# Building one-hot rows on another engine, turning a product's layout in PSUM, and keeping more low parts in DRAM

## The chip, the cores and the metric

One core of one Trainium2 chip runs the whole kernel. The metric is device time in microseconds (us) of one execution. Before the change the median is 3289.25 us (3288.27 and 3289.25 in two runs of three; a third gave 9417.04). The profiled execution took 3298.0 us, of which the trace spans 3296.2 us.

## The reference

One decoder layer over 1024 tokens of width 1024: a mixer of two branches (RG-LRU and gated linear attention), a projection and a layer norm, then a PEER layer (product keys over 128 x 128 = 16384 single-neuron experts, 8 heads, 16 experts a head) beside a gated projection of per-layer embeddings, and a second layer norm.

```python
z = x @ w_in;  m = sigmoid(g_A) * y_A + sigmoid(g_B) * y_B
x = layer_norm(ALPHA * x + m @ w_out)
ple = sigmoid(x @ W_pg) * (p @ W_pp)
top_s, top_i = top_k(scores of 2 x 128 half keys, 16)          # per head
best_s, best_pos = top_k(16 x 16 sums, 16); gate = softmax(best_s)
hid = gelu(x . u[expert]);  ffn = sum over 128 slots of gate * hid * v[expert]
x = layer_norm(ALPHA * x + ffn + ple)
```

Everything is float32 in and out.

## The kernel before

The tokens go through the mixer and what follows it in two halves of 512 (`mixer(0)`, `post(0)`, `mixer(1)`, `post(1)`), and then `dense` ends the program. Each large product is made of three products of rounded halves (`mm3`, L263 to L265): an operand is split into a high part (ScalarE, L259) and a low part (VectorE subtraction, L260). `weights` (L267 to L287) does this for every weight block, once in each half. The first 60 low parts are also written to DRAM (L286) in the first half and read from there in the second half (L277), where only the high part is then made (L278). In the second half the remaining ones, four blocks of `w_out` (`mix`), eight of the queries (`pq`), eight of the embedding gate (`plg`) and four of its projection (`plp`), are split again.

The experts are computed in two ways. Four of the eight tiles of 128 tokens gather rows of `u` and `v` by indirect DMAs from the GpSimd queue: `gather_u` (L841) takes one expert per token and slot, and VectorE multiplies and sums it (L849); `gather_v` (L857) takes the 128 experts of one token, and TensorE sums them with a weight tile `w32` that is zero but for one column per token (L866, L869). The rows go round in a ring of 7 tiles, 11 later on. The other four tiles are dense: `dense` multiplies them by all 16384 experts, a group of 512 at a time, and multiplies the hidden values by a gate matrix (`gt`, L1042) that lies in DRAM as `g_d`.

`dense_gates` (L962 to L994) builds that matrix while `post(1)` runs. For one token the 128 slots lie on the partitions. One one-hot matrix marks each slot's first key and is scaled by the slot's gate (`oi`), the other marks its second key (`oj`), and their product over the slots (L988) gives 128 x 128 gates. A group is 8 tokens: one VectorE instruction makes eight bare rows of first keys (`one`, L979), one makes eight of second keys (`oj`, L981), ScalarE scales `one` token by token into `oi` (L987), TensorE makes eight products into two PSUM tiles, and ScalarE copies each tile to `gst` with tokens turned innermost (L990). Sixteen tokens go to DRAM in one store (L992). There are 64 groups.

The order of the work: the code is written in one order, and gather work is woven in by `pump`, which hands out a fixed amount of it after each product. A scheduler with its own timing model then orders the instructions of every engine. Each engine, and each of the two DMA queues (SyncE's and GpSimd's), takes its instructions in that order. `dense` may start before the gates are finished, but its first use of the gate matrix (L1042) needs the last store.

## Time and profile before

| What | before |
|---|---|
| median of the runs | 3289.25 us |
| profiled execution | 3298.0 us |
| its span | 3296.2 us |
| TensorE busy | 3042.8 us (92%) |
| VectorE busy | 2375.3 us (72%) |
| ScalarE busy | 1228.2 us (37%) |
| GpSimd busy | 1160.8 us (35%) |
| moved by DMA | 939.74 MB, mean 285 GB/s |

Shares of the whole span hide stages that differ. The program has five: the first mixer, the rest of the first half (some 440 to 640 us), the second mixer (to 1100), the rest of the second half with the gates (1100 to 1632), the dense experts (1632 to 3257), and a tail. A stage is read by its own row of busy times, and then by the waits inside it. Busy time of TensorE counts a matmul longer when the granted clock is low.

### The profile page before, as it was taken

How to read it: one execution, taken by the hardware profiler on the slowest of the kernel's cores; microseconds unless marked ns; L12 is line 12 of the kernel's file. 1: busy time of each engine (PE TensorE's matmuls, PEld its weight loads, DVE VectorE, ACT ScalarE, POOL GpSimd, SP SyncE). 2: the span in 40 equal slices, each digit the busy share in tenths (PEclk: the TensorE clock that was granted, in tenths of full speed). 3: DMA queues.
4: the chain of work that ended last, by engine and by line, in shares of the span. 5: the costliest groups of instructions: out<-in, count | busy, mean ns of one | idle time of the engine just before them, and what ended most of it. 6: DMA issues, size and time to landing. Idle time of an engine off the chain costs nothing.

```text
span 3296.2 us, 48127 instructions
## 1 busy us (share of the span) xinstructions
PE 3042.8 (92%) x17160; PEld 2320.6 (70%) x17160; DVE 2375.3 (72%) x5791; ACT 1228.2 (37%) x2130; POOL 1160.8 (35%) x1034
## 2 busy tenths in 40 slices
PE   8999989797999888658799999999999999999996
PEld 6788777676777676548577777777777777777663
DVE  7556557977888898978887866666666667666333
ACT  6433323263244464648623322222232232223221
POOL 0000000534421445540155444444434545443453
PEclk9999989898999998879899999999999999999997
DMA  5444444777776898976799899999899999988997
GB/s 174 143 172 148 135 160 142 277 293 284 295 263 244 326 312 302 349 252 216 246 376 352 321 338 327 340 338 344 314 340 326 355 335 326 338 328 327 346 322 277
DMA packets 364304, 939.74 MB, mean 285 GB/s; under 512 B 33920, under 2 KB 115968, under 8 KB 359968
## 3 DMA queue, kind: packets, MB, share of 16 engines
q0 software_dynamic: 147456, 536.94, 44.8%
q1 hardware_dynamic: 216608, 399.74, 34.8%
q8 instruction: 134, 2.20, 0.3%
q14 instruction: 106, 0.87, 0.1%
HBM read 854.76 MB, written 81.79 MB: 284 GB/s over the span
## 4 chain that ended last, share of the span: by engine, by line
PE 70%; DVE 14%; DMA 7%; ACT 4%; issue 3%; POOL 1%; SPq 0%; POOLq 0%; DVEq 0%; ACTq 0%
PE ph L263 7%; PE ph L265 7%; PE pv L265 7%; PE pv L263 7%; PE pv L264 7%; PE ph L264 7%; PE ffn L883 7%; DVE ug L849 3%; DMA ug<-in_peer_u_dram,idx 3%; DMA vg<-in_peer_v_dram,idxT 1%; DVE one L979 1%; DVE oj L981 1%; PE pgr L263 1%; PE pgr L264 1%; PE pgr L265 1%
## 5 line engine op out<-in xcount | busy, mean ns | idle before, releaser
L847 POOL DMA_INDIRECT ug<-in_peer_u_dram,idx x512 | 601.3, 1174 | 1345.1 <-DVE bs L776 612.3
L876 POOL DMA_INDIRECT vg<-in_peer_v_dram,idxT x512 | 558.2, 1090 | 756.7 <-DVE ug L849 324.3
L849 DVE SCALAR_TENSOR_TENSOR ug<-ug,x1g 128x1024 f32<-128x1024 f32 x512 | 619.8, 1219 | 47.0 <-DMA ug<-in_peer_u_dram,idx 42.9
L263 PE MATMUL ph<-x1hl,uh 128*128 128x512 f32 x1024 | 408.6, 399 | 0.9 <-DVE sc L737 0.9
L265 PE MATMUL ph<-x1hl,ul 128*128 128x512 f32 x1024 | 407.9, 398 | 0.0
L264 PE MATMUL ph<-x1hl,uh 128*128 128x512 f32 x1024 | 406.6, 397 | 0.0
L264 PE MATMUL pv<-vl,wdh 128*128 128x512 f32 x1024 | 400.5, 393 | 0.0
L263 PE MATMUL pv<-vh,wdh 128*128 128x512 f32 x1024 | 384.3, 393 | 15.9 <-ACT wdh L259 15.9
L265 PE MATMUL pv<-vh,wdl 128*128 128x512 f32 x1024 | 398.7, 393 | 0.0
L259 ACT ACTIVATE uh<-ur 128x512 fp32r<-128x512 f32 x256 | 160.2, 628 | 498.0 <-PE ph L264 489.2
L883 PE MATMUL ffn<-vg,w 128*32 128x512 f32 x2048 | 274.1, 628 | 51.1 <-DMA vg<-in_peer_v_dram,idxT 50.2
L259 ACT ACTIVATE vh<-vr 128x512 fp32r<-128x512 f32 x256 | 160.7, 629 | 356.9 <-PE pv L265 348.7
L260 DVE TENSOR_TENSOR ul<-ur,uh 128x512 fp32r<-128x512 f32 x256 | 175.7, 687 | 159.6 <-ACT uh L259 158.1
L260 DVE TENSOR_TENSOR vl<-vr,vh 128x512 fp32r<-128x512 f32 x256 | 176.3, 690 | 115.2 <-ACT vh L259 115.0
L1062 DVE SCALAR_TENSOR_TENSOR acc<-acc,pv 128x512 f32<-128x512 f32 x256 | 165.0, 681 | 108.8 <-PE pv L265 108.8
L263 PEld LDWEIGHTS pv<-vh,wdh 128*128 128x128 f32 x1024 | 192.8, 188 | 69.3 <-ACT wdh L259 16.1
L263 PEld LDWEIGHTS ph<-x1hl,uh 128*128 128x128 f32 x1024 | 192.4, 188 | 68.6 <-issue 22.6
L265 PEld LDWEIGHTS ph<-x1hl,ul 128*128 128x128 f32 x1024 | 192.4, 188 | 62.1 <-issue 16.8
L265 PEld LDWEIGHTS pv<-vh,wdl 128*128 128x128 f32 x1024 | 192.6, 188 | 58.7 <-issue 16.8
L264 PEld LDWEIGHTS ph<-x1hl,uh 128*128 128x128 f32 x1024 | 192.4, 188 | 55.7 <-issue 11.7
L264 PEld LDWEIGHTS pv<-vl,wdh 128*128 128x128 f32 x1024 | 192.9, 188 | 53.9 <-issue 10.1
L988 PE MATMUL pg<-oi,oj 128*128 128x128 f32 x1024 | 163.2, 301 | 35.9 <-ACT oi L987 25.4
(475 smaller groups left out, 6030.9 us busy)
## 6 DMA issues: line engine op xcount, KB each, us to landing
ur<-in_uT_dram SPq DMA_DIRECT2D x256, 256.0 KB, 6.3
vr<-in_peer_v_dram SPq DMA_DIRECT2D x256, 256.0 KB, 6.3
g_d<-gst SPq DMA_DIRECT2D x32, 1024.0 KB, 8.6
gt<-g_d SPq DMA_DIRECT2D x32, 1024.0 KB, 8.4
raw_zx<-in_w_z_dram SPq DMA_DIRECT2D x16, 512.0 KB, 4.9
raw_zv<-in_w_v_dram SPq DMA_DIRECT2D x16, 512.0 KB, 5.0
raw_zy<-in_w_z_dram SPq DMA_DIRECT2D x16, 512.0 KB, 6.4
raw_ga<-in_w_z_dram SPq DMA_DIRECT2D x16, 512.0 KB, 5.4
```

The lines of the kernel that those rows point to most:

```text
L259: nc.scalar.activation(h, src, AF.Copy)
L260: nc.vector.tensor_tensor(l, src, h, op=ALU.subtract)
L263: nc.tensor.matmul(o, wh, xh, start=first, stop=False)
L264: nc.tensor.matmul(o, wh, xl, start=False, stop=False)
L265: nc.tensor.matmul(o, wl, xh, start=False, stop=last)
L847: nc.gpsimd.indirect_dma_start(out=ug, out_offset=None, in_=a["peer_u"], in_offset=bass.IndirectOffsetOnAxis(ap=idx[:, s:s + 1], axis=0))
L849: nc.vector.scalar_tensor_tensor(ug, ug, 1.0, x1, op0=ALU.mult, op1=ALU.mult, accum_out=hid[:, s:s + 1])
L876: nc.gpsimd.indirect_dma_start(out=vg, out_offset=None, in_=a["peer_v"], in_offset=bass.IndirectOffsetOnAxis(ap=idxT[:, t:t + 1], axis=0))
L883: mm = nc.tensor.matmul(ffn[32 * c:32 * c + 32, e * 512:(e + 1) * 512], w32[:, c, r], rows_v[c][:, e * 512:(e + 1) * 512], start=ph == 0 a ...
L979: nc.vector.tensor_tensor(one, iota, Tb[:, 0, tt, None].to_broadcast(B3), op=ALU.is_equal)
L988: nc.tensor.matmul(o[:, r], oj[:, t], oi, start=True, stop=True)
L1062: nc.vector.scalar_tensor_tensor(acc[c][:, es], acc[c][:, es], 0.5 if g == 0 else 1.0, o[c], op0=ALU.mult, op1=ALU.add)
```

## The change

Five edits:

1. `oi` is made by VectorE, one instruction a token, which compares a row of key numbers with the slot's first key and multiplies by its gate, both read from one column of `T2`. ScalarE no longer makes it.
2. `one` now marks the second key and is laid key, token (128 x 8) so that both inputs and the output are bfloat16 with neighbouring elements next to each other. ScalarE turns it into `oj` (token, key, float32) with one instruction a group. VectorE's `oj` is gone.
3. The product of a token goes into every fourth column of its PSUM tile, which is laid key, token (128 x 4). The copy to `gst` then reads PSUM as it lies and writes four neighbouring values at a time.
4. In `gather_v` the zero fill of `w32` moves from VectorE to GpSimd, and its four small copies move to ScalarE.
5. `LOW = 60` is gone. All low parts but those of the queries (`OWN`) are kept in DRAM: 16 more writes in the first half and 16 more reads in the second, in place of 16 subtractions.

```diff
-LOW = 60
+OWN = ("pq",)
...
-            if key not in low:
-                n = len(low)
-                low[key] = None
-                if n < LOW:
-                    low[key] = dram.tile(shape, F32, name=f"low{n}")
-                    nc.sync.dma_start(low[key], l.bitcast(F32))
+            if name not in OWN and key not in low:
+                low[key] = dram.tile(shape, F32, name=f"low{len(low)}")
+                nc.sync.dma_start(low[key], l.bitcast(F32))
...
-            nc.vector.memset(w32, 0.0)
+            nc.gpsimd.memset(w32, 0.0)
             for c in range(4):
...
-                nc.vector.tensor_copy(dst, pw[:, 32 * c + ph * N:32 * c + ph * N + N])
+                nc.scalar.activation(dst, pw[:, 32 * c + ph * N:32 * c + ph * N + N], AF.Copy)
...
-                one = g_b.tile(B3, BF16, name="one", bufs=2)
-                nc.vector.tensor_tensor(one, iota, Tb[:, 0, tt, None].to_broadcast(B3), op=ALU.is_equal)
-                oj = g_b.tile(B3, F32, name="oj", bufs=2)
-                nc.vector.tensor_tensor(oj, iota, Tb[:, 1, tt, None].to_broadcast(B3), op=ALU.is_equal)
+                one = late.tile([P, KEYS, TG], BF16, name="one", tag="k_", bufs=2)
+                nc.vector.tensor_tensor(one, iota, Tb[:, None, t0:t0 + TG].to_broadcast([P, KEYS, TG]), op=ALU.is_equal)
+                oj = g_b.tile([P, TG, KEYS], F32, name="oj", bufs=2)
+                nc.scalar.activation(oj.rearrange("p t k -> p k t"), one, AF.Copy)
+
+                oi = g_b.tile([P, TG, KEYS], F32, name="oi", bufs=2)
+                for t in range(TG):
+                    nc.vector.tensor_scalar(oi[:, t], iota128, T2[:, 0, t0 + t:t0 + t + 1], T2[:, 1, t0 + t:t0 + t + 1],
+                                            op0=ALU.is_equal, op1=ALU.mult)
                 for r4 in range(TG // 4):
-                    o = gps.tile([P, 4, KEYS], F32, name="pg", tag="g")
+                    o = gps.tile([P, KEYS, 4], F32, name="pg", tag="g")
                     for r in range(4):
                         t = 4 * r4 + r
-                        oi = g_b.tile([P, KEYS], F32, name="oi", bufs=6)
-                        nc.scalar.activation(oi, one[:, t], AF.Copy, scale=T3[:, 2, t0 + t:t0 + t + 1])
-                        nc.tensor.matmul(o[:, r], oj[:, t], oi, start=True, stop=True)
+                        nc.tensor.matmul(o[:, :, r], oj[:, t], oi[:, t], start=True, stop=True)
                     q4 = q * TG + 4 * r4
-                    nc.scalar.activation(gs[:, :, q4:q4 + 4].rearrange("p i t -> p t i"), o, AF.Copy)
+                    nc.scalar.activation(gs[:, :, q4:q4 + 4], o, AF.Copy)
```

The scheduler orders the changed program anew. On VectorE, among the queries of the second half, a piece of the gates read as follows (`list` and `sc_st` belong to the top 16 of the scores, `ug` is a gathered row):

```order
1988 L979 TENSOR_TENSOR one<-iota,Tb 128x1024
1989 L737 MATCH_REPLACE sc_st<-list_11488,sc_st 128x128 x2
1990 L739 MAX_INDEX list_11488<-list_11488,sc_st 128x8
1991 L737 MATCH_REPLACE sc_st<-list_11488,sc_st 128x128
1992 L849 SCALAR_TENSOR_TENSOR ug,hid<-ug,x1g 128x1024
1993 L737 MATCH_REPLACE sc_st<-list_11488,sc_st 128x128
1994 L260 TENSOR_TENSOR wl_pq<-raw_pq,wh_pq 128x1024
1995 L981 TENSOR_TENSOR oj<-iota,Tb 128x1024
```

The same place of the changed kernel:

```order
2028 L981 TENSOR_SCALAR oi<-iota_145,T_11591 128x128 x8
2029 L975 TENSOR_TENSOR one<-iota,Tb 128x1024
2030 L846 SCALAR_TENSOR_TENSOR ug,hid<-ug,x1g 128x1024
2031 L734 MATCH_REPLACE sc_st<-list_11408,sc_st 128x128 x4
2032 L732 MAX list_11408<-sc_st 128x8 x4
2033 L981 TENSOR_SCALAR oi<-iota_145,T_11591 128x128 x6
2034 L735 MAX list_11408<-sc_st 128x8 x4
```

Where a group had two instructions of 1024 elements, it now has one of 1024 and eight of 128, in runs of up to eight.

On ScalarE, further on in the same stage, the gates stood so:

```order
762 L990 ACTIVATE gst<-pg 128x4x128
763 L987 ACTIVATE oi<-one,T_13031 128x128 x4
764 L990 ACTIVATE gst<-pg 128x4x128
765 L987 ACTIVATE oi<-one,T_13031 128x128 x4
766 L990 ACTIVATE gst<-pg 128x4x128
```

And now:

```order
679 L977 ACTIVATE oj<-one 128x128x8
680 L989 ACTIVATE gst<-pg 128x128x4
681 L977 ACTIVATE oj<-one 128x128x8
682 L989 ACTIVATE gst<-pg 128x128x4
683 L977 ACTIVATE oj<-one 128x128x8
684 L989 ACTIVATE gst<-pg 128x128x4
```

Eight scalings and two copies of a group have become one turning copy and two copies.

On TensorE, at the end of the gates, the first products of the dense stage (`ph`) were mixed with the last of the gates (`pg`); 96 of them stood ahead of the last piece:

```order
6146 L264 MATMUL ph<-x1hl,uh 128x512
6147 L265 MATMUL ph<-x1hl,ul 128x512
6148 L988 MATMUL pg<-oi,oj 128x128 x36
6149 L263 MATMUL pv_15402<-vh,wdh 128x512
6150 L264 MATMUL pv_15402<-vl,wdh 128x512
```

In the changed kernel none does:

```order
6026 L264 MATMUL pplp_14634<-wl_plp,Ehl 128x256
6027 L265 MATMUL pplp_14634<-wh_plp,Ehl 128x256
6028 L987 MATMUL pg<-oi,oj 128x128 x8
6029 L263 MATMUL ph<-x1hl,uh 128x512
6030 L264 MATMUL ph<-x1hl,uh 128x512
```

The dense stage's products now follow the last product of the gates, and 36 of them stand ahead of the first `pv`.

## Rows read from the trace of the kernel before

**Rows 1.** Windows by stage: length, busy us (instructions) of each engine, clock, DMA

```profile
440.00:640.00 200.00, 164.98 (x1072) 147.53 (x1073) 155.74 (x589) 49.61 (x80) 30.35 (x24) 0.88 0.52 176
1100.00:1632.00 532.00, 408.26 (x2702) 335.69 (x2701) 477.53 (x1342) 340.70 (x771) 204.90 (x158) 0.88 0.86 291
1632.00:3257.00 1625.00, 1625.00 (x7725) 1171.16 (x7724) 1073.01 (x2134) 457.61 (x767) 765.86 (x713) 1.00 0.92 335
3257.00:3296.00 39.00, 9.59 (x53) 1.75 (x49) 17.07 (x27) 1.36 (x5) 4.69 (x5) 0.56 0.62 228
```

**Rows 2.** Groups by line, VectorE, 1100 to 1632 us: busy, mean ns | idle before

```profile
L849 DVE SCALAR_TENSOR_TENSOR ug<-ug,x1g 128x1024 f32<-128x1024 f32 x81 | 98.3, 1219 | 22.8 <-DMA ug<-in_peer_u_dram,idx 20.5 <-issue 2.1
L981 DVE TENSOR_TENSOR oj<-iota,Tb 128x1024 f32<-128x1024 bf16 x64 | 77.7, 1214 | 4.6 <-PE pg L988 4.6
L979 DVE TENSOR_TENSOR one<-iota,Tb 128x1024 bf16<-128x1024 bf16 x64 | 77.6, 1212 | 13.4 <-ACT oi L987 13.3
L260 DVE TENSOR_TENSOR wl_plg<-raw_plg,wh_plg 128x1024 fp32r<-128x1024 f32 x8 | 9.7, 1213 | 0.5 <-ACT wh_plg L259 0.4
```

**Rows 3.** Groups by line, ScalarE, 1100 to 1632 us

```profile
L987 ACT ACTIVATE oi<-one,T 128x128 f32<-128x128 bf16 x512 | 165.0, 390 | 41.2 <-DVE one L979 21.1 <-PE pg L988 19.9
L990 ACT ACTIVATE gst<-pg 128x512 f32<-128x512 f32 x128 | 133.3, 1054 | 14.0 <-DMA g_d<-gst 9.6 <-PE pg L988 4.2
L683 ACT ACTIVATE sc_st<-psc 128x512 f32<-128x512 f32 x16 | 8.8, 595 | 4.2 <-DVE list L739 4.2
```

**Rows 4.** Waits of TensorE and its weight loads, 1100 to 1632 us: total, times, longest

```profile
PE ffn L883 <- DMA vg<-in_peer_v_dram,idxT: 39.6, 9, 12.2
PE pgb L265 <- DMA wl_gb<-low: 1.1, 1, 1.1
...
PEld pg L988 <- ACT oi L987: 46.6, 45, 4.7
```

**Rows 5.** Groups by line, whole span: shapes that the change uses

```profile
L260 DVE TENSOR_TENSOR vl<-vr,vh 128x512 fp32r<-128x512 f32 x256 | 176.3, 690 | 115.2 <-ACT vh L259 115.0
L809 DVE TENSOR_TENSOR eq<-rb,iota 128x1024 bf16<-128x1024 bf16 x32 | 22.0, 688 | 0.5
L866 DVE MEMSET w<- 128x512 f32 x32 | 15.5, 485 | 26.1 <-PE ffn L883 25.2
```

**Rows 6.** Timeline of VectorE: start, length; 128 elements, constants in the instruction

```profile
575.36 0.22 DVE L785 TENSOR_SCALAR rk<-bp 128x128 uint32<-128x128 uint32 x1
575.49 0.22 DVE L786 TENSOR_SCALAR rk<-bp 128x128 uint32<-128x128 uint32 x1
```

**Rows 7.** Timeline of VectorE: L166 reads a value per partition, 32 elements

```profile
3.60 0.17 DVE L162 TENSOR_SCALAR ish<-irow 128x32 int32<-128x32 int32 x1
3.71 0.24 DVE L166 TENSOR_SCALAR lmask<-i_f,jf 128x32 f32<-128x32 f32 x1
3.87 0.15 DVE L167 TENSOR_SCALAR jsh<-jsh 128x1 int32<-128x1 int32 x1
```

**Rows 8.** Timeline of TensorE: gate products, and two products of the dense stage

```profile
1126.19 2.02 PE L988 MATMUL pg<-oi,oj 128*128 128x128 f32 x16 [0.94 <-DVE oj L981]
...
3210.40 0.39 PE L263 MATMUL ph<-x1hl,uh 128*128 128x512 f32 x1
3210.63 0.39 PE L264 MATMUL ph<-x1hl,uh 128*128 128x512 f32 x1
```

**Rows 9.** Timeline at the end of the gates

```profile
1611.28 1.07 PE L988 MATMUL pg<-oi,oj 128*128 128x128 f32 x6 [0.60 <-ACT oi L987]
...
1628.21 0.80 PE L263 MATMUL pv<-vh,wdh 128*128 128x512 f32 x1 [15.86 <-ACT wdh L259]
```

**Rows 10.** Waits, whole span: the store of the gated embeddings

```profile
ACT tge L716 <- DMA base_d<-tge: 26.0, 3, 15.7
```

**Rows 11.** The chain that ended last, its tail: start, length, what

```profile
3262.25 11.20 DMA vg<-in_peer_v_dram,idxT
3273.49 3.69 PE ffn L883 x16
```

More of the change, by code (lines that the diff above doesn't have):

```diff
@@ L967, in dense_gates @@
             nc.tensor.transpose(o[:, j], K3[:, j], ident)
-        T3 = g_b.tile([P, 3, P], F32, name="T3", bufs=2)
-        nc.scalar.activation(T3, o[:, :3], AF.Copy)
-        Tb = g_b.tile([P, 2, P], BF16, name="Tb", bufs=2)
-        nc.scalar.activation(Tb, o[:, :2], AF.Copy)
+        T2 = g_b.tile([P, 2, P], F32, name="T2", bufs=2)
+        nc.scalar.activation(T2, o[:, 0:3:2], AF.Copy)
+        Tb = g_b.tile([P, P], BF16, name="Tb", bufs=2)
+        nc.scalar.activation(Tb, o[:, 1], AF.Copy)
         for tb in range(P // 16):
@@ L975, in dense_gates @@
                 t0 = tb * 16 + q * TG
-                tt = slice(t0, t0 + TG)
-                B3 = [P, TG, KEYS]
-                one = g_b.tile(B3, BF16, name="one", bufs=2)
-                nc.vector.tensor_tensor(one, iota, Tb[:, 0, tt, None].to_broadcast(B3), op=ALU.is_equal)
-                oj = g_b.tile(B3, F32, name="oj", bufs=2)
-                nc.vector.tensor_tensor(oj, iota, Tb[:, 1, tt, None].to_broadcast(B3), op=ALU.is_equal)
+                one = late.tile([P, KEYS, TG], BF16, name="one", tag="k_", bufs=2)
[6 more added lines that the diff above has]
+                                            op0=ALU.is_equal, op1=ALU.mult)
                 for r4 in range(TG // 4):
-                    o = gps.tile([P, 4, KEYS], F32, name="pg", tag="g")
+                    o = gps.tile([P, KEYS, 4], F32, name="pg", tag="g")
                     for r in range(4):
                         t = 4 * r4 + r
-                        oi = g_b.tile([P, KEYS], F32, name="oi", bufs=6)
-                        nc.scalar.activation(oi, one[:, t], AF.Copy, scale=T3[:, 2, t0 + t:t0 + t + 1])
-                        nc.tensor.matmul(o[:, r], oj[:, t], oi, start=True, stop=True)
+                        nc.tensor.matmul(o[:, :, r], oj[:, t], oi[:, t], start=True, stop=True)
                     q4 = q * TG + 4 * r4
-                    nc.scalar.activation(gs[:, :, q4:q4 + 4].rearrange("p i t -> p t i"), o, AF.Copy)
+                    nc.scalar.activation(gs[:, :, q4:q4 + 4], o, AF.Copy)
                     pump(0.9)
@@ L1106 @@
         gps = gctx.enter_context(tc.tile_pool(name="gps", bufs=3, space=PSUM))
-        iota = late.tile([P, TG, KEYS], BF16, name="iota", tag="tr")
-        nc.scalar.activation(iota, iota128[:, None, :].to_broadcast([P, TG, KEYS]), AF.Copy)
+        iota = late.tile([P, KEYS, TG], BF16, name="iota", tag="tr")
+        nc.scalar.activation(iota, iota128[:, :, None].to_broadcast([P, KEYS, TG]), AF.Copy)
         def all_gates():
```

## The prediction, made before the run

> **What bounds the kernel now.** I read the windows by stage first [rows 1]. From 1632 to 3257 us TensorE is busy for all of 1625 us at full clock: whatever is taken off VectorE, ScalarE or GpSimd there is worth nothing, and the edits of `w32` fall there for the most part. The stage that can give time back is the one with the gates, 1100 to 1632 us. TensorE is busy for 408 of its 532 us, ScalarE for 341, GpSimd for 205, and VectorE for 478. So VectorE bounds it on average, with 54 us of idle time, and TensorE has 124 us in which it waits.
>
> The groups and waits of that stage say for what. VectorE's idle time is 20.5 us of waiting for gathered rows, and 13.3 and 4.6 us before `one` and `oj` for ScalarE and TensorE to give a buffer back [rows 2]. TensorE's weight loads wait 46.6 us for ScalarE's `oi`, and its sums wait 39.6 us for gathered rows [rows 4]. ScalarE spends 165.0 + 133.3 = 298 of its 341 us on `oi` and `gst` [rows 3]. There are thus two things in the way, not one: VectorE's total, and ScalarE as the slow link between VectorE's rows and TensorE's products.
>
> **VectorE's part of the gates.** A group has `one` and `oj`, 1212 and 1214 ns [rows 2], 2.43 us. Now `one` has the shape, types and neighbouring elements of the comparison at L809, 0.69 us [rows 5]. Each `oi` is an instruction of 128 elements that reads two values per partition. No row shows exactly that. With constants in the instruction, 128 elements start 0.13 us apart [rows 6]; that is the lower end. Reading one value per partition lengthens an instruction of 32 elements from 0.17 to 0.24 us, and the next starts after 0.16 us [rows 7]; 96 more elements, at the rate that the 0.22 us of 128 elements against 0.17 us of 32 gives, add 0.05 us. That makes 0.24 + 0.05 = 0.29 us if nothing overlaps, the upper end, and 0.16 + 0.05 = 0.21 us if it overlaps as rows 7 do, which I take because they are the nearest. A group: 0.69 + 8 x 0.21 = 2.37 us against 2.43, so **-4 us** in 64 groups, with **-45 us** (0.13) and **+37 us** (0.29) as ends. VectorE's share of the gates hardly gets smaller; it changes shape.
>
> **ScalarE's part.** A group costs 8 x 0.390 + 2 x 1.054 = 5.23 us [rows 3]. The copy to `gst` writes every value 64 bytes from the last, and took 1054 ns where a copy of the same size that writes neighbours took 595 [rows 3]. I price the new `oj`, twice the size and with steps of 512 bytes, at 2 x 1.054 = 2.1 us (2 x 0.595 = 1.2 us below), and the new `gst`, four neighbours at a time, at 0.595 (1.054 above): 3.3 us a group, between 2.4 and 4.2. In 64 groups ScalarE gives up some 124 us (66 to 181) of its 341. All of it lies beside VectorE's work, so it counts only by the waits that it ends: VectorE's 13.3 + 4.6 us [rows 2], **-18 us**. TensorE's 46.6 us for `oi` go too, but are not added, since VectorE's rows come no sooner.
>
> **Low parts.** In the second half 12 splits of 1024 elements (1.213 us, [rows 2]) and four of 512 (0.690, [rows 5]) leave VectorE: **-17 us**, in the stage that it bounds. In their place SyncE's queue gets 16 reads, 7.3 MB by their shapes. Such reads made TensorE wait 1.1 us once in this stage [rows 4]; I take **+2 us** for 16. In the first half the queue gets 16 writes, next to the stores of `base_d`. The transfers have room there (a share of 0.52, [rows 1]), but the queue is taken in order, and a store that is late holds up ScalarE, which already waited 26.0 us for it [rows 10]. Below nothing; above, each write puts off what stands behind it by its 0.5 MB at 335 GB/s [rows 1], 16 x 1.5 = 24 us. I take **+5 us**: TensorE waits 35 of 200 us there, so not all is hidden.
>
> **`w32`.** Some five of the 32 zero fills lie in this stage (161 of 1024 sums stand ahead of the gates' end in either order), 5 x 0.485 [rows 5] = **-2 us**. The small copies I leave out. GpSimd has 327 us free there, and the fill's wait for a buffer is one that the gather behind it has too: with 11 row tiles, neither goes ahead before the same sum is done. In the dense stage GpSimd is busy for 766 of 1625 us and ScalarE for 458 [rows 1]; a copy that waits on ScalarE delays the splits behind it, which TensorE's loaded blocks cover by some microseconds. If that cover were gone, the 27 later fills would show as gaps in a TensorE that has none.
>
> **Order.** No dense product stands ahead of the last gate any more, so 14 of VectorE's dense splits (0.690, [rows 5]) and some seven dot products (1.219, [rows 2]) move behind it: **-18 us** before that point, into a stage where VectorE has room. In return TensorE had done 96 products at 0.23 us [rows 8], 22 us of work, before the last gate; it then sat idle for 15.9 us [rows 9] until the store, the load of `gt` and `w` were through. Now it can fill that wait with what it had done ahead: I take 5 us of idle time left, so 22 - 15.9 + 5 = **+11 us**. In the tail, 24 sums stood behind the last `pv` and 8 do now: two batches, at half of the 3.69 us that 16 took [rows 11], **-4 us**.
>
> **The sum.** -4 - 18 - 17 + 2 + 5 - 2 - 18 + 11 - 4 = -45 us. One thing pushes back: the same gathers in less time. The stage moves 291 GB/s at a share of 0.86 where the dense stage reaches 335 at 0.92 [rows 1], so 532 x 291 / 335 = 462 us is the least that its transfers allow. They do not bind, but VectorE's 20.5 us of waiting for rows will grow; by half, **+10 us**. Together -35 us. The profiled execution took 3298.0 us, 8.75 above the median of 3289.25, and by its own time would come to 3263. Put to the median, **3254 us**.
>
> **Rivals.**
> - *VectorE takes back what ScalarE gives up.* If eight `oi` in a run do not overlap (0.29 us), VectorE has 41 us more and the sum is +6: 3295 us. For it: the 0.15 to 0.24 us that each instruction takes even when it has almost nothing to do [rows 7], and eight where there were none. Against: every row in the list starts before the one ahead has ended. Chance 0.22.
> - *The values per partition cost nothing.* At 0.13 us: -41 more, 3213 us. For it: rows 6. Against: rows 7. Chance 0.15.
> - *TensorE becomes the bound and the kernel slower.* A gate product now writes every fourth column. 16 halves of products took 2.02 us [rows 8], so one starts every 0.116 us, and there are 1024. TensorE has 124 us of waiting, of which 44 for rows and low parts would stay; the other 80 cover a spacing of up to 0.116 + 80/1024 = 0.19 us, and from there it decides. At twice, 0.232 us, it lacks 39 us: 3289 + 39 + 5 - 4 = 3329 us, if the edits of VectorE give nothing more. Against: a dense product writes 512 neighbouring columns in 0.23 us [rows 8], two in the 0.9 ns in which a gate product writes one, so the gate product leaves each write twice the time. For it: no row shows a spread write. Chance 0.08.
> - *The reads of low parts end nothing because VectorE has other work that holds the same step.* Then the -17 us fall away: 3271 us. Chance 0.05.
>
> [...]
>
> **How the numbers follow.** The forecast, 3254 us, has 0.5, with some 20 us either way for the terms that I only took. The range reaches to the ends of `oi`'s price and 5 us past the upper one, for the terms taken: **3213 to 3300 us**, which leaves out the third rival and what lies past either end, 2 in 10. A difference of 2% (66 us) is about what can be told from no change, so faster is below 3223: most of the second rival and the low edge of the forecast, **0.17**. Slower is above 3355: only a spread write at more than twice the spacing, **0.03**. Within: **0.80**.
>
> **What would show it.** In the profile after: `oi` on VectorE at about 0.29 us busy one by one and 0.21 from start to start; `one` at 0.69; `oj` on ScalarE at about 2 us and `gst` near 0.6; TensorE's `pg` still 0.116 us apart; no wait of `pg` for ScalarE of more than a few microseconds; VectorE as busy as before in the gates' stage, which ends some 40 us sooner, with a stage of 1625 us behind it that has not changed. Wrong would be: gaps in TensorE in the dense stage, `pg` spaced wider, or a first half that is longer by more than 10 us.

## The result, and the profile after

The changed kernel took **3309.89 us** (median of 7 runs), the kernel before beside it 3295.72: the ratio is **1.0053** (95% interval 1.0036 to 1.0070). It is slower by 0.5%, far from the 2% that counts as a difference, and outside the forecast range of 3213 to 3300. The ratio compares the means and leaves out one slow run of the kernel before, of 9417.04 us. A second measurement gave 1.0027 (1.0014 to 1.0040): the sign holds, the size varies. The profiled execution took 3316.68 us with a span of 3314.9, 18.7 us more than the span before.

The steps of the stage can be read from one view, by tile: count, ns of one (min/median/max), first and last start. After:

```profile
L987 PE MATMUL pg<-oi,oj x1024: 270/275/582, 1135.5 to 1594.2; 128*128 128x128 f32 x171
L265 PE MATMUL pplp<-wh_plp,Ehl x64: 276/281/415, 566.1 to 1592.4; 128*128 128x256 f32 x64
L263 PE MATMUL pv<-vh,wdh x1024: 387/389/747, 1638.0 to 3290.2; 128*128 128x512 f32 x171
L880 PE MATMUL ffn<-vg,w x2048: 592/592/1062, 1081.6 to 3293.7; 128*32 128x512 f32 x187
```

(`pg` are the gate products, `pplp` those of the embeddings, `pv` the first of the dense stage that use the gates, `ffn` the sums of gathered rows.) Before, the first gate product started at 1126.2 us, the last at 1612.1, the first `pv` at 1628.2 [rows 8, 9], and the last embedding product at 1542.7:

```profile
L265 PE MATMUL pplp<-wh_plp,Ehl x64: 276/279/415, 564.9 to 1542.7; 128*128 128x256 f32 x64
```

The 18.7 us are then:

| stretch | before | after | difference | forecast |
|---|---|---|---|---|
| up to the first gate product | 1126.2 | 1135.5 | +9.3 | +5 |
| first to last gate product | 485.9 | 458.7 | -27.2 | -47 |
| last gate product to first `pv` | 16.1 | 43.8 | +27.7 | +7 with the next row |
| first `pv` to the end | 1668.0 | 1676.9 | +8.9 | |
| sum | | | +18.7 | -35 |

The gates do end 18 us sooner. The hand-over to `dense` takes all of that back and more. Two windows of before (columns as in [rows 1]), from the first gate product to the last and from there to the first `pv`:

```profile
1126.20:1612.10 485.90, 382.32 (x2571) 315.93 (x2571) 438.85 (x1208) 322.58 (x744) 188.60 (x143) 0.89 0.86 287
1612.10:1628.20 16.10, 0.25 (x2) 0.06 (x1) 14.35 (x81) 3.74 (x6) 3.81 (x4) 0.54 0.76 268
```

And after; the first row is the rest of the first half, the other two are the same stretches as above:

```profile
440.00:640.00 200.00, 163.04 (x1053) 145.20 (x1053) 157.45 (x595) 50.24 (x80) 30.42 (x23) 0.88 0.61 208
...
1135.00:1594.20 459.20, 351.46 (x2475) 296.92 (x2475) 410.88 (x1486) 244.63 (x302) 152.82 (x141) 0.86 0.88 294
1594.20:1638.00 43.80, 12.30 (x56) 8.11 (x54) 22.54 (x89) 5.64 (x9) 16.96 (x15) 0.69 1.00 360
```

In the gates VectorE is busy for 411 of 459 us; over the same stretch before it was 438.9 of 485.9. Its idle time, 47 us before and 48 after, has not moved: the stretch got shorter by just what VectorE was relieved of. The groups say why that was less than hoped. VectorE, 1100 to 1638 us (busy, mean ns | idle before them):

```profile
L981 DVE TENSOR_SCALAR oi<-iota,T 128x128 f32<-128x128 f32 x496 | 136.9, 350 | 14.4 <-PE pg L987 11.4 <-ACT T L966 3.0
L846 DVE SCALAR_TENSOR_TENSOR ug<-ug,x1g 128x1024 f32<-128x1024 f32 x83 | 100.4, 1224 | 28.6 <-DMA ug<-in_peer_u_dram,idx 25.8 <-issue 1.6 <-DMA vg<-in_peer_v_dram,idxT 0.8
L975 DVE TENSOR_TENSOR one<-iota,Tb 128x1024 bf16<-128x1024 bf16 x64 | 42.8, 682 | 5.9 <-ACT oj L977 5.9
```

ScalarE in the same stretch:

```profile
L977 ACT ACTIVATE oj<-one 128x1024 f32<-128x1024 bf16 x64 | 129.7, 2042 | 11.2 <-DVE one L975 11.1
L989 ACT ACTIVATE gst<-pg 128x512 f32<-128x512 f32 x128 | 74.7, 605 | 72.2 <-PE pg L987 56.0 <-DMA g_d<-gst 15.6 <-ACT gst L989 0.3
```

`one`, `oj` and `gst` cost what was forecast: 0.68, 2.04 and 0.605 us against 0.69, 2.1 and 0.595. ScalarE's two groups take 204 us in place of 298 [rows 3]. Only `oi` is off, as the timeline shows at the end of the gates (start, length, count):

```profile
1589.42 2.14 DVE L981 TENSOR_SCALAR oi<-iota,T 128x128 f32<-128x128 f32 x8
1591.47 0.76 DVE L720 SCALAR_TENSOR_TENSOR tge<-y,tge 128x256 f32<-128x256 f32 x2
...
1592.52 1.95 PE L987 MATMUL pg<-oi,oj 128*128 128x128 f32 x16
```

Eight `oi` keep VectorE for 2.05 us until the next instruction starts, 0.257 each; the forecast took 0.21. Sixteen gate products, which now write every fourth column, take 1.95 us against 2.02 [rows 8], both at a granted clock of 1.00: a spread write costs TensorE nothing here.

Waits of TensorE and its weight loads in 1100 to 1638 us (total, times, longest):

```profile
PE ffn L880 <- DMA vg<-in_peer_v_dram,idxT: 39.8, 6, 16.3
...
PE ph L263 <- ACT uh L259: 27.0, 1, 27.0
PEld pg L987 <- ACT oj L977: 17.5, 11, 5.2
...
PE pplg L264 <- DMA wl_plg<-low: 13.3, 5, 5.9
...
PE pv L263 <- ACT vh L259: 4.5, 1, 4.5
```

The weight loads waited 46.6 us for `oi` [rows 4] and now wait 17.5 for `oj`; new are 13.3 us for low parts read from DRAM, and one wait of 27.0 us for `uh`, the first weights of `dense`. The timeline of that wait, on SyncE's queue, ScalarE and TensorE:

```profile
1598.79 6.74 SPq L721 DMA_DIRECT2D base_d<-tge  x2
1609.90 0.80 SPq L1026 DMA_DIRECT2D gt<-g_d  x2
1610.87 1.86 SPq L1010 DMA_DIRECT2D ur<-in_uT_dram  x3
...
1620.82 0.63 ACT L259 ACTIVATE uh<-ur 128x512 fp32r<-128x512 f32 x1 [25.72 <-DMA ur<-in_uT_dram]
...
1621.51 0.80 PE L263 MATMUL ph<-x1hl,uh 128*128 128x512 f32 x1 [27.04 <-ACT uh L259]
```

The last embedding product (1592.4) leads to the last store of `base_d` (issued by 1605.5), and behind that stand the load of `gt` and only then the first dense weights, which need 10 us more at a DMA share of 0.98. The load of `gt` itself waits for the gates' last store to land, the last 4.2 us of it with nothing else on the queue, and by GpSimd's wait the last store of `base_d` had landed at 1610.8: the two things that can hold `ur` end within 1 us of each other here, and this trace alone does not tell them apart. Before, the embeddings were over at 1542.7, 69 us ahead of the last gate product; after, 1.8 us. In the kernel before, `ur` had landed long ago by then (the first `ph` started at 1559.1), 96 products of `dense` were done, and TensorE idled for 15.9 us [rows 9].

### The profile page after: what moved, and what is told of

The parts are those of the page before. It is cut to its first block, busy times and chain, and to the rows that moved or that the text cites. A ratio compares the mean times of both kernels' runs of the same rounds, so it can differ in the third digit from the quotient of the medians.

```text
span 3314.9 us, 48143 instructions
## 1 busy us (share of the span) xinstructions
PE 3039.6 (92%) x17160; PEld 2318.8 (70%) x17160; DVE 2362.8 (71%) x6063; ACT 1168.2 (35%) x1810; POOL 1155.7 (35%) x1066
## 4 chain that ended last, share of the span: by engine, by line
PE 71%; DVE 14%; DMA 8%; ACT 4%; issue 3%; POOL 1%; SPq 0%; DVEq 0%; ACTq 0%; POOLq 0%
PE ph L265 7%; PE ph L263 7%; PE ph L264 7%; PE ffn L880 7%; PE pv L264 7%; PE pv L263 7%; PE pv L265 7%; DVE ug L846 3%; DMA ug<-in_peer_u_dram,idx 2%; DVE oi L981 1%; DMA wl_plg<-low 1%; PE pg L987 1%; PE pgr L263 1%; PE pgb L265 1%; PE pgb L264 1%
## 5 line engine op out<-in xcount | busy, mean ns | idle before, releaser
L844 POOL DMA_INDIRECT ug<-in_peer_u_dram,idx x512 | 582.9, 1138 | 1392.4 <-DVE idxT L831 597.2
L1041 DVE TENSOR_TENSOR w<-w,gt 128x256 f32<-128x256 f32 x256 | 97.5, 421 | 127.7 <-ACT w L1038 127.7
```

The costliest lines, as they stand in the source:

```text
L844: nc.gpsimd.indirect_dma_start(out=ug, out_offset=None, in_=a["peer_u"], in_offset=bass.IndirectOffsetOnAxis(ap=idx[:, s:s + 1], axis=0))
L1041: nc.vector.tensor_mul(wq, wq, G[i // 8][q][:, :, i % 8])
```

## Theories and experiments

- **Theory A**, the hand-over: the dense loads stand behind the embeddings' last store, and the embeddings now end with the gates; so `dense` starts late whatever the gates do.
- **Theory B**, the price: 512 `oi` cost VectorE more than was forecast, and VectorE holds the gates.
- **Theory C**, the low parts: their writes and reads cost more than the splits that they replace.

All ratios are to the kernel before on the same chip, with 95% intervals; lengths are from the profiles as in the table above. "Hand-over" is last gate product to first `pv`, "emb. to pv" last embedding product to first `pv`.

| run | ratio | gates, us | VectorE busy in them | hand-over | emb. to `pv` | `pv` to end |
|---|---|---|---|---|---|---|
| before (twice) | 1 | 485.9, 483.9 | 439, 438 | 16.1, 16.1 | 86, 87 | 1668, 1667 |
| the change (twice) | 1.0053, 1.0027 | 458.7, 458.4 | 410, 411 | 43.8, 43.9 | 46, 46 | 1677, 1677 |
| e1 gates alone | 1.0044 (1.0029 to 1.0058) | 473.5 | 429 | 47.0 | 45 | 1670 |
| e2, e14 low parts and w32 | 0.9945, 0.9951 | 454.5, 451.6 | 407, 408 | 24.0, 24.0 | 54, 52 | 1673, 1672 |
| e3 embeddings first | 0.9992 (0.9976 to 1.0007) | 473.4 | 419 | 21.4 | 47 | 1681 |
| e4 half of `oi` | 0.9907 (0.9878 to 0.9935) | 433.5 | 361 | 32.7 | 36 | 1674 |
| e12 `oi` by constants | 0.9967 (0.9955 to 0.9980) | 415.9 | 359 | 68.5 | 55 | 1673 |
| e7, e15 low parts alone | 1.0047, 1.0004 | 476.6, 478.0 | 414, 414 | 21.5, 21.5 | 59, 59 | 1668, 1669 |
| e13 change with 60 low parts | 1.0089 (1.0073 to 1.0106) | 481.0 | 428 | 56.7 | 53 | 1666 |
| e10 w32 alone | 1.0000 (0.9985 to 1.0016) | 486.0 | 430 | 17.8 | 68 | 1672 |
| e9 layout alone | 0.9953 (0.9928 to 0.9977) | 470.8 | 435 | 17.2 | 83 | 1668 |
| e8 w32 and layout | 0.9967 (0.9948 to 0.9986) | 477.4 | 429 | 19.1 | 70 | 1673 |
| e5 layout, low parts, w32 | 0.9961 (0.9949 to 0.9973) | 449.7 | 406 | 24.1 | 54 | 1673 |
| e6 mixed one-hots | 0.9975 (0.9963 to 0.9987) | 438.7 | 369 | 30.1 | 45 | 1673 |
| e11 mixed, 60 low parts | **0.9923** (0.9897 to 0.9950) | 463.8 | 401 | 19.8 | 68 | 1669 |
| e16 e11, embeddings first | 0.9933 (0.9909 to 0.9958) | 465.4 | 401 | 26.5 | 75 | 1668 |

Kernels that were profiled twice show the same lengths to 3 us, so these lengths carry the argument. The start of the first gate product is not among them: it moved by 2 to 10 us between two profiles of one kernel (1135.5 and 1144.2 us in the change). The ratio of one kernel moved by up to 0.4% between chips (e7 and e15), more than its intervals say, and no ratio here reaches the 2% that counts as a difference.

**e1, the gates' edit alone.** The kernel before with the new `one`, `oj`, `oi`, `pg` and `gst`, and nothing else.

> The kernel before with the edit of the gates alone (one, oi, oj, the product's layout, gst). Theory A (the hand-over to the dense stage): the loss comes with this edit, because the scheduler then puts every dense load behind the last store and the load of gt on SyncE's queue; TensorE should again sit idle for some 25 us before the first ph, and the time be 10 to 25 us above before. Theory B (price of the one-hot rows): VectorE has 29 us more to do for the gates (141 + 43 against 155), the last pg comes no sooner than before (1612 us or later), and the loss is there, not in the hand-over. Theory C (low parts): this kernel is no slower than before, since the waits for wl_plg are not in it.

Measured 1.0044. The gates' stretch is 12 us shorter, the hand-over 31 us longer: by itself the edit has both halves of the result, and TensorE waits 31.3 us for the first dense weights. The last gate product comes at 1611.9 us, where Theory B had it, but from a start at 1138.4. The last store of `base_d` and the load of `gt` again stand ahead of the first dense weights on SyncE's queue:

```profile
1614.78 6.98 SPq L724 DMA_DIRECT2D base_d<-tge  x4
1626.46 0.80 SPq L1029 DMA_DIRECT2D gt<-g_d  x2
1627.35 3.23 SPq L1071 DMA_DIRECT2D acc<-base_d  x2
1630.93 1.28 SPq L1013 DMA_DIRECT2D ur<-in_uT_dram  x3
```

**e2, the other two edits alone** (the change with the gates as before; repeated as e14).

> The changed kernel with the old gates: only the low parts and w32 changed. A: nine dense loads stand ahead of gt on the queue, so the hand-over is nearly that of before, TensorE's wait before ph is below 5 us, and the saved 17 us of splits make it 0 to 15 us faster than before. C: the reads of low parts make TensorE wait some 13 us for wl_plg, and it is 5 to 20 us slower than before.

0.9945, and 0.9951 on another chip: without the gates' edit the change would have been half a per cent below the kernel before. With e1, which has the loss without them, Theory C falls as the cause of the loss.

**e3, embeddings first.** In the change, the embeddings' products of a block are emitted ahead of the gates of that block:

```
-            block(j)
...
+            block(j)
```

> The changed kernel, with each block of the gates placed in the program behind the embedding products of its block instead of ahead of them; same work. Six dense loads then stand ahead of gt on SyncE's queue instead of none, and the embeddings no longer end the stage. A: TensorE's wait before ph falls from 27 us to below 8 us and the time by 10 to 25 us against the changed kernel, to that of before or a few us below. B: the wait may go, but the last pg moves back by as much, and the time stays within 5 us of the changed kernel's.

The hand-over fell from 44 to 21 us and the waits for the first dense weights from 27 to 10 us, as Theory A says, but the gates took 15 us of that back, and 4 us went behind. 0.9992 is 0.35 to 0.6% better than the change. The order costs something, but moving the embeddings is paid in part by the gates. TensorE's waits (1080 to 1680 us) have one of that size:

```profile
PE pg L987 <- ACT gst L989: 15.1, 3, 9.9
```

The change has no such wait. `gst` in turn waited for the gates' own stores, 25.0 us in place of 15.6, and these alternate on SyncE's queue with the embeddings' stores and reads. That would account for the 15 us, but no run took it apart.

**e4, half of `oi`.** Four rows of `oi` are made in a group and each is used by two tokens; the other half is left out.

```
-                oi = g_b.tile([P, TG, KEYS], F32, name="oi", bufs=2)
-                for t in range(TG):
+                oi = g_b.tile([P, TG // 2, KEYS], F32, name="oi", bufs=2)
+                for t in range(TG // 2):
...
-                        nc.tensor.matmul(o[:, :, r], oj[:, t], oi[:, t], start=True, stop=True)
+                        nc.tensor.matmul(o[:, :, r], oj[:, t], oi[:, t // 2], start=True, stop=True)
```

> The changed kernel with four instead of eight oi a group, each used by two tokens; half of the scaled one-hot rows are left out. VectorE has 256 x 0.275 = 70 us less to do in the stage. B: the last pg comes 40 to 70 us sooner and the whole time falls by as much. A: the last pg comes sooner only as far as VectorE held it, but the dense loads still stand behind the last embedding store (three of them ahead of gt), so the idle time before ph stays above 15 us and the gain is below 40 us.

256 instructions less, 66 us at 0.257, made the gates 25 us shorter, not the 40 to 70 that Theory B expected, and the time 1.2 to 1.5% better than the change's. Another 11 us came from the hand-over: six dense loads now stand ahead of `gt`. B holds: `oi` on VectorE is on the path, though not to the full.

**e12, the same number of `oi`, without pointers.** The values of the gates are left out: each `oi` is made from two constants in the instruction.

```
-                    nc.vector.tensor_scalar(oi[:, t], iota128, T2[:, 0, t0 + t:t0 + t + 1], T2[:, 1, t0 + t:t0 + t + 1],
+                    nc.vector.tensor_scalar(oi[:, t], iota128, 7.0, 0.5, op0=ALU.is_equal, op1=ALU.mult)
```

> The change with oi made from two constants in place of the two per-partition columns (the same 512 instructions of 128x128 fp32, so the gates' values are left out). Theory B (the pointers are the price): 0.275 us from start to start falls to 0.13 (the row with constants in the kernel before), 512 x 0.145 = 74 us off VectorE, about what leaving half the instructions out took (70 us, ratio 0.9907): 0.988 to 0.993. If 128 elements of fp32 cost 0.27 whatever the scalars are, the time stays at the change's 1.005.

The timeline of VectorE has the second of a pair 0.13 us behind the first, as [rows 6] did:

```profile
1356.19 0.35 DVE L981 TENSOR_SCALAR oi<-iota 128x128 f32<-128x128 f32 x2
...
1356.71 0.36 DVE L981 TENSOR_SCALAR oi<-iota 128x128 f32<-128x128 f32 x2
```

So the two values per partition cost 0.257 - 0.13 = 0.127 us an instruction, 65 us in 512, and without them the gates are 43 us shorter. The time fell by 0.6 to 0.9% only, short of the expected gain, and the tiles show why:

```profile
L986 PE MATMUL pg<-oi,oj x1024: 269/275/582, 1140.9 to 1556.8; 128*128 128x128 f32 x171
...
L265 PE MATMUL pplp<-wh_plp,Ehl x64: 276/281/416, 567.4 to 1570.7; 128*128 128x256 f32 x64
...
L263 PE MATMUL pv<-vh,wdh x1024: 387/389/794, 1625.3 to 3275.7; 128*128 128x512 f32 x171
```

The gates are over 14 us ahead of the embeddings, and the first `pv` still comes 55 us behind these. That is Theory A without help from B: with one-hots as in the change, `pv` starts 45 to 55 us behind the last embedding product (e4: 36), however early the gates end. Here the loads of `gt` were issued by 1579 us, so they hold nothing up, and what the first dense loads (L1009) waited for stands in SyncE's waits (1555 to 1615 us) and in the chain that ended last (start, length):

```profile
SPq L1009 <- DMA base_d<-tge: 5.0, 1, 5.0
...
1581.21 18.68 DMA base_d<-tge
...
1600.80 12.01 DMA ur<-in_uT_dram
```

The loads go out only when the last store of `base_d` has landed, 18.7 us after its issue, at a DMA share of 1.01 over the hand-over. The same wait stands before them in the kernel before (1.9 us, at 1550), e3 (4.3), e4 (1.3) and e13 (5.0). The program opens the dense stage's tiles only after it has closed those of the embeddings, so the loads most likely wait for that memory; no run gave them memory of their own.

**e5, layout, low parts and w32** (the change with `one`, `oj` and `oi` as before, but the products laid key, token).

> Low parts, w32 and the gates' PSUM layout of the change, with the gates' one-hots as before (one and oj by VectorE at 1.21 us, oi by ScalarE at 0.32 us each). It is the run with one-hots as before plus one edit: the products are written with key then token inside the bank, and the copy gst reads and writes 16-byte pieces. Theory B (the row price on VectorE is the fault of the change, and the layout is its good part): gst falls from 1.06 us to 0.60 us, 128 of them, 58 us less on ScalarE, PE's waits for oi and gst (35 us in the run without this edit) fall by 15 to 30, so 3265 to 3285 us here, ratio 0.985 to 0.991. Theory A (the hand-over decides): dense loads stand ahead of the load of gt again, 96 ph products go ahead, so no worse than 0.9945, but also no better than 0.992, since the stretch is held by the embeddings and not by ScalarE. If writes with a step in PSUM slow the fp32 products, pg's spacing leaves 0.12 us and the ratio goes over 0.998.

The ratio, 0.9961, falls short of what either theory expected, 0.985 to 0.991 and 0.992 to 0.9945. In the profile the stretch of the gates is 2 to 5 us shorter than in e2 and e14, with the same hand-over; VectorE's idle time there, 43 us, is e14's (44): ScalarE's 58 us ended no wait of the engine that holds the stage.

**e9, the layout alone.**

```
-                    o = gps.tile([P, 4, KEYS], F32, name="pg", tag="g")
+                    o = gps.tile([P, KEYS, 4], F32, name="pg", tag="g")
...
-                        nc.tensor.matmul(o[:, r], oj[:, t], oi, start=True, stop=True)
+                        nc.tensor.matmul(o[:, :, r], oj[:, t], oi, start=True, stop=True)
...
-                    nc.scalar.activation(gs[:, :, q4:q4 + 4].rearrange("p i t -> p t i"), o, AF.Copy)
+                    nc.scalar.activation(gs[:, :, q4:q4 + 4], o, AF.Copy)
```

> The kernel before with the PSUM layout of the products alone: ScalarE's copy gst 128 x (1.05 - 0.59) = 59 us less, nothing else. Theory B (prices): PE's waits for oi and gst in the gates (25 us before) fall by 10 to 20, ratio 0.993 to 0.997. A rival, that VectorE (90 to 98 per cent busy in 1180 to 1380 us) holds that stretch and ScalarE's relief ends nothing: 0.998 to 1.002.

0.9953 in one measurement, inside Theory B's range: three lines of the change are worth half a per cent by themselves, about as much as a ratio moves between chips. The gates' stretch, 13 to 15 us shorter, carries it. ScalarE's groups in 1100 to 1628 us:

```profile
L987 ACT ACTIVATE oi<-one,T 128x128 f32<-128x128 bf16 x512 | 169.0, 393 | 60.2 <-DVE one L979 32.0 <-PE pg L988 20.8 <-issue 5.8
L990 ACT ACTIVATE gst<-pg 128x512 f32<-128x512 f32 x128 | 74.6, 587 | 16.8 <-DMA g_d<-gst 8.0 <-PE pg L988 7.4 <-PE pplg L263 0.7
```

`gst` takes 587 ns for 1054 [rows 3], and VectorE's idle time in the gates falls from 46 to 36 us: this is the relief of ScalarE that the prediction counted at -18, and here, where VectorE's own work stays as it was, 10 us of it do come.

**e8, w32 and layout**, and **e10, w32 alone**, on the kernel before.

```
-            nc.vector.memset(w32, 0.0)
+            nc.gpsimd.memset(w32, 0.0)
...
-                nc.vector.tensor_copy(dst, pw[:, 32 * c + ph * N:32 * c + ph * N + N])
+                nc.scalar.activation(dst, pw[:, 32 * c + ph * N:32 * c + ph * N + N], AF.Copy)
```

> The kernel before with two edits of the change: w32 (memset by GpSimd, copies by ScalarE) and the gates' PSUM layout (gst 0.59 us in place of 1.05). Low parts of 60 blocks as before, one-hots as before. If the writes of 16 more low blocks are what cost the 9 us ahead of the gates, the first ffn begins again at 1071 to 1075 us on a chip like that of the last runs, and the ratio is 0.986 to 0.992, best of all. Theory A: 12 dense loads go ahead of the load of gt and the embeddings end by 1555 us; the same range. If it is the planner's order alone and no price, anything between 0.992 and 1.004.

> The kernel before with the w32 edit alone. Forecast -2 us: 0.998 to 1.001. If w32 is what made the run with low parts and w32 fast (0.9945) while low parts alone are slow (1.0047), then 0.988 to 0.994, with 29 memsets of 0.485 us and about as many groups of copies less on VectorE in 1080 to 1640 us, 20 to 25 us of the engine that is fullest there.

w32 alone is worth nothing (1.0000), as forecast (-2 us). With the layout it gave 0.9967, no better than the layout alone and short of the 0.986 to 0.992 expected. Its first `ffn` began at 1079.6 us, not at 1071 to 1075. The second range expected for e10 had no ground: in 1080 to 1640 us the kernel before has 5 zero fills (2.4 us) and 20 small copies (2.0 us) on VectorE, not 29 fills.

**e7 and e15, the low parts alone**, on the kernel before.

```
-            if key not in low:
-                n = len(low)
-                low[key] = None
-                if n < LOW:
...
+            if name not in OWN and key not in low:
```

> The kernel before with the edit of the low parts alone (all but the queries' kept, 28 of 32 stored weights read back in place of the split). The sum of the forecast had -17 for splits, +2 for reads, +5 for writes: -10 us, ratio 0.997. Theory C (the low parts lose: writes of more blocks take DMA time in 400 to 640 us, reads make pplg wait) expects 1.001 to 1.005, and the first ffn late by 5 to 10 us against the kernel before on this chip. Theories A and B: 0.994 to 0.998, with the dense loads still ahead of gt (10 of them).

> Low parts alone, again, on the chip of the pair. If 1.0047 is its own, 1.003 to 1.007; if the pair's gain is the chip's, 0.994 to 0.998.

1.0047 and 1.0004; the second lies in neither of the ranges expected for it. Part of their cost lies ahead of the gates. By the tile view of 1060 to 1100 us (columns as in the first one) the first sum of gathered rows starts at 1073.2 us in the kernel before, profiled again on that chip:

```profile
L883 PE MATMUL ffn<-vg,w x32: 590/592/617, 1073.2 to 1097.7; 128*32 128x512 f32 x32
```

and 9.2 us later in e7, by the same view:

```profile
L880 PE MATMUL ffn<-vg,w x16: 589/592/617, 1082.4 to 1083.8; 128*32 128x512 f32 x16
```

So on that chip the low parts cost 9 us there. The other kernels with the 16 further low parts began 2 to 12 us later than one with 60 on their chip, and kernels with 60 began anywhere from 1071.8 to 1082.2 us on different chips. In the change the sum starts at 1081.6 us: how much of its +9.3 us is the low parts' and how much the chip's is not shown. What the writes add is seen in 440 to 640 us, where the DMA share is 0.61 against 0.52 [rows 1]. VectorE is busy for 25 us less in the gates, but these get only 7 us shorter, and the hand-over 5 us longer.

**e13, the change with 60 low parts as before**, and **e14**, the pair of e2 again.

> The change with the low parts of 60 blocks as before: gates and w32 alone. If low parts lose by themselves (0.47% alone), 0.999 to 1.003 here. If they gain (0.55% with w32), 1.006 to 1.012. Gates alone were 1.0044, w32 alone 1.000, so 1.003 to 1.006 by adding those two.

> Low parts and w32 with the gates as before, again. If 0.9945 was the pair's own, 0.993 to 0.997. If it was the chip's, 1.002 to 1.006, as for low parts alone.

1.0089: inside the change the low parts gain, 22 us in the gates and 13 in the hand-over against 11 us behind the first `pv` and some 6 us ahead of the gates (the first `ffn` starts at 1075.4 us in e13 and at 1081.8 in e12, on one chip). The reads are not free. The chain that ended last in the change runs through them (start, length):

```profile
1445.85 14.71 DMA wl_plg<-low
1473.23 12.10 DMA base_d<-tge
1512.13 10.02 DMA wl_plg<-low
1598.25 11.52 DMA g_d<-gst
1614.97 18.01 DMA acc<-base_d
```

**e6 and e11, mixed one-hots.** First keys as bf16 laid key, token by VectorE, second keys as fp32 by VectorE as before, `oi` by ScalarE from the first; products laid key, token. e11 also keeps only 60 low parts.

```
+                nc.vector.tensor_tensor(one, iota[0], Tb[:, 0, None, tt].to_broadcast(BK), op=ALU.is_equal)
...
+                nc.vector.tensor_tensor(oj, iota[1], Tb[:, 1, tt, None].to_broadcast(B3), op=ALU.is_equal)
...
+                        nc.scalar.activation(oi, one[:, :, t], AF.Copy, scale=T3[:, t0 + t:t0 + t + 1])
```

> As the change, with the one-hots dealt out otherwise: first keys as bf16 by VectorE laid key, token (0.68 us for 8 tokens), second keys as fp32 by VectorE laid token, key (1.21 us), and the 512 scaled rows by ScalarE from the first with a step of 16 bytes. VectorE's gates 64 x (0.68 + 1.21) = 121 us against 184 in the change and 155 before; ScalarE's 165 (if the stepped read costs nothing) + 75 = 240 us against 204 and 298. Theory B: both engines have less than before, so the gates' waits fall and the time is 3270 to 3295 us, ratio 0.986 to 0.994. Theory A: the hand-over is between the two (6 dense loads ahead of gt, 72 products ahead of the first pv), so 0.992 to 0.999. If the stepped read costs ScalarE 0.1 us a row, 50 us come back there: ratio 0.997 to 1.004.

> The mixed one-hots (VectorE 121 us, ScalarE 512 x 0.52 + 74 = 303 us by the run with them) with low parts of 60 blocks as before. Against that run, whose ratio was 0.9975, the low parts' 9 us ahead of the gates and some of the hand-over come back: 0.992 to 0.996. If the low parts have no part in it, 0.996 to 0.999.

e6 came to 0.9975, below the gain that Theory B expected and inside Theory A's range, and e11 to 0.9923, as expected the lowest of the kernels that compute all the gates, though the intervals of several others (e2, e9, e14, e16) overlap with its own. ScalarE's stepped read is not free, as e6 shows:

```profile
L985 ACT ACTIVATE oi<-one,T 128x128 f32<-128x128 bf16 x512 | 228.6, 523 | 33.5 <-PE pg L986 24.3 <-DVE one L976 9.2
L988 ACT ACTIVATE gst<-pg 128x512 f32<-128x512 f32 x128 | 73.5, 589 | 3.7 <-PE pg L986 3.2 <-DMA g_d<-gst 0.3
```

523 ns against 390 [rows 3], 68 us in 512 on an engine that has room for them. The gates of e6 are 20 us shorter than the change's.

**e16, e11 with embeddings first**, and the change again.

> The mixed one-hots with low parts of 60 blocks, and a block's gates emitted behind its embeddings, as in the run of the change with embeddings first. Theory A: 96 products and 14 dense loads go ahead again and the embeddings' last store comes by 1550 us; 0.986 to 0.992 against 0.9923 without the edit. If VectorE and ScalarE hold the stage by now, the gates end later by as much as the embeddings end sooner: 0.991 to 0.996.

> The change again: 1.003 to 1.008, with 500 to 506 us from the first gate product to the first product of pv and a wait for the first dense weights of 20 to 30 us.

0.9933, outside Theory A's range: nothing more is gained. In e11 and e16 alike the embeddings end 48 us ahead of the last gate product; they no longer set the start of `dense`, and Theory A has nothing left to win. The change again gave 458.4 us of gates, 43.9 of hand-over and a wait of 27.9 us for the first dense weights; its ratio, 1.0027, lay just under the range. The kernel before again:

> The kernel before, unchanged, for its profile on this chip beside the others. If the 9 us that the change lost ahead of its gates are the chip's, the first ffn begins here at 1078 to 1084 us and not at 1072 us; if they are the change's, at 1070 to 1074 us.

It began its first `ffn` at 1073.2 us, inside the range for a loss that is the change's; but the change profiled again began at 1086.4 us and e16, with 60 low parts and on the same chip as that, at 1082.2: the chip has a part in it too.

## Why the prediction was wrong

It named the right stage and the right engines, and three of the four new prices were right. The sum was 53.7 us off, at three places.

**The step "Order" failed, by 30 us of 54.** It put +7 on what lies behind the last gate product (22 - 15.9 + 5 - 4), and +36.6 came. It held that TensorE would fill the wait with the 96 products that it had formerly done ahead, with 5 us of idle time left; it idled for 31.5 us (43.80 less 12.30 in the window above), and these 26.5 us are nearly all of the 30. The order showed that no dense product stood ahead of the last gate any more, and the prediction counted what that moves, but did not ask what those products wait for: their weights, whose loads now stand behind the embeddings' last store and behind `gt` on SyncE's queue. e1 has the same 47 us by the gates' edit alone, e12 has 68.5 us with gates that end 14 us ahead of the embeddings, and there the loads wait for the embeddings' last store and not for `gt`; e3 brings it to 21 us, though 15 us of that came back in the gates. Why the scheduler lets the embeddings end so late once `oi` is VectorE's work stays open.

**The price of `oi` failed, by 9 to 16 of the 20 us that the gates missed.** It was taken at 0.21 us from start to start, between the ends 0.13 and 0.29; it is 0.257. A group costs 0.68 + 8 x 0.257 = 2.74 us against 2.43, +20 us in 64 groups in place of -4. By what VectorE's time is worth in the gates (25 us for 66 in e4, 43 for 65 in e12) these 24 us make those 9 to 16. This was the first rival's direction, at 0.22: 0.257 lies a little nearer its 0.29, but its 3295 us left the hand-over out.

**ScalarE's relief (-18) ended no wait.** VectorE's waits before `one` and `oj`, 17.9 us [rows 2], are now 5.9 before `one` and 14.4 before `oi`, and its idle time in the gates is the same. The `oj` that ScalarE turns in 2.04 us is a link in the chain as the eight scaled rows were: the weight loads wait 17.5 us for it. e9 shows 10 us of the term for the layout by itself; beside the low parts and `w32` (e5 against e14) the layout left VectorE's idle time as it was. The +10 us for gathered rows came as +5, 25.8 us of waiting against 20.5 [rows 2]; the 335 GB/s behind it are not the most that the transfers reach, since the hand-over moved 360.

**The low parts** were priced at -10 in all: -17, +2, +5. Ahead of the gates +9.3 came for the +5, of which the chip has a part that is not known; in the gates TensorE waited 13.3 us for reads in place of 2, with 7 to 15 us from one read's issue to its landing in the chain. Even so they gain inside the change (e13 1.0089 against 1.0053 and 1.0027).

**Right were** `w32` (nothing measurable), a dense stage that is as full as before (TensorE idles for 3.6 of 1654 us behind the first `pv`), and the third rival's refutation: gate products, 128x128 in fp32 and now writing every fourth value, still start 0.11 us apart (16 in 1.95 us, against 2.02 before [rows 8]), where the rival needed 0.232 to be worth its 39 us. The second rival (pointers that cost nothing) is refuted by e12.

**What stays open:** why the low parts gain 0.5% with `w32` (twice), yet nothing or a loss without (twice), where `w32` alone is worth nothing. VectorE's busy time in the gates differs by 6 to 7 us, the length by 22 to 26. The orders differ in many places at once, and no run took them apart.

## What to carry to other kernels

When a change ends one stage sooner, follow what the next stage's first instruction waits for, down to its load and to what that load stands behind on its queue; the end of the stage before it is often another chain than the one that the change relieves. A per-instruction price between two ends wants a row with the same operands: with constants in place of the two values per partition the change measured 0.9967, with them 1.0027 and 1.0053. And of a change with several edits, run each alone and in pairs: here the three lines of the layout gave 0.5% by themselves and nothing beside the low parts and `w32`.

## What the runs showed of the hardware

- A VectorE instruction of 128 fp32 elements takes 0.257 us from start to start with two per-partition values (the change), 0.13 with constants (e12).
- ScalarE writes 1024 fp32 values 512 bytes apart in 2.04 us, about as long as two copies of 512 values that go 64 bytes apart (1.054 each [rows 3]); 16-byte pieces go at the pace of neighbours (0.587 us in e9 and 0.605 in the change for 512, against 0.595 [rows 3]). It reads 128 bf16 values 16 bytes apart in 523 ns, neighbours in 390 (e6).
- fp32 products of 128x128 that write every fourth PSUM value start 0.11 us apart (16 in 1.95 us), those that write neighbours 0.12 us (16 in 2.02 us [rows 8]), both at a granted clock of 1.00. A 128x512 product of `ph` is 0.63 us long at a granted clock of 0.50 and 0.40 us at 1.00 (the change, 1622.0 to 1624.2 and 1624.6 to 1628.6 us).
- At a DMA share of 1.01 (e12's hand-over) a store of 128 KB took 18.7 us to land and a load of 256 KB 12.0 us. At 0.98 the change's first dense load, also 256 KB, took 10 us, where the median of the change's 256 such loads is 6.2 us.
